# Summing 32,768 rows on one core: the first row joins a six-row load, narrower matmul pieces, the result stored in two parts from one partition

## The chip, the cores and the metric

The kernel runs on one core of one Trainium2 chip. The metric is the device time of an execution in microseconds; smaller is better. Medians are compared only with the kernel before on the same chip and in the same rounds. The profiled execution shows a span of its own, some 2 us shorter than the device time.

## The reference, cut to what matters

```python
def setup_inputs():
    batch, seq, dim = 32, 1024, 2048
    return {"grad_output": np.random.randn(batch, seq, dim).astype(np.float32)}

def reference(grad_output):
    return np.sum(grad_output, axis=(0, 1)).astype(np.float32)
```

32,768 rows of 2048 fp32 values are summed to one row. In the kernel a "row" is a block of 128 array rows, one on each partition (1 MB); there are 256 of them.

## The kernel before

The vector engine folds thirty 8-row tiles into a few rows in SBUF. The tensor engine adds up the partitions of what is left, with a column of ones as the stationary operand, into PSUM; it also takes the last rows straight from their loads: the vector engine is busy with the others without a pause from 567.16 to 618.00 us (trace). All loads are issued by one queue, in this order (a lane is the place of one row in the ring buffer):

```python
LEFT = ((0, 512, 0), (512, 512, 1), (1024, 512, 2))     # first column, columns, strip of the array
RIGHT = ((1536, 256, 2), (1792, 256, 3))
...
load(1, head[:], head_in)                               # one row first, for the vector engine
for k in range(TILES):                                  # 30 tiles of 8 rows, three buffers
    s = k % SLOTS
    load(TILE, rows(s * TILE, TILE), slot_in[s], (vec, k - 2) if k >= SLOTS else None)
load(1 + LANES, rows(0, 1 + LANES), rows_in, (vec, TILES - 2))   # five rows for the tensor engine
load(SMALL, rows(small_at, SMALL), small_in, (vec, TILES - 1))   # four rows for the vector engine
for j in range(LANES):
    load(1, rows(j, 1), row_in[j], (used, j + 1))       # one row each, once the lane is given back
...                                                     # then two rows, left columns before right
```

The tensor engine's program is 44 matmuls: one row, a loop body of four rows (run twice), the vector engine's sum, and the two last rows. A row is one matmul per piece; in the loop each row has a filler matmul besides, whose result is not used.

```python
matmuls(LANES * D, LEFT + RIGHT, wait=(rows_in, 16), start=True)
with nc.tensor.Fori(0, ROUNDS):
    for j, lane in enumerate(row_in):
        take(nc.tensor, lane)
        nc.tensor.matmul(psum[96:97, 1024:1024 + FILLER], ...)      # filler
        matmuls(j * D, LEFT + RIGHT).then_inc(used, 1)
matmuls(at * D, LEFT + RIGHT, wait=(step, n_step))
for x, lo, pieces, lane, stop in final:
    matmuls(x, pieces, lo, wait=(lane, 16), then=...)
```

Then the sums are copied out of PSUM and stored, left on partitions 0, 32 and 64, right on partition 96, by one DMA of four 2 KB pieces.

## Time and profile before

| | before |
|---|---|
| median of the first three runs | 629.28 us |
| span of the profiled run | 627.5 us |
| DMA engines taken | 99.1% |
| vector engine busy | 532.3 us |
| last load landed (trace) | 623.25 us |
| store started / landed (trace) | 624.46 / 626.22 us |

How to read it: the DMA engines are full from 2 us to 622 us, so the time is that of 268 MB plus a start of 2 us and an end of 4 to 5 us. "Landed" is the moment at which the sixteenth increment of a load's completion semaphore is recorded (each load gets sixteen; that each comes from another of the 16 DMA engines is assumed).

### The profile page before, as it was taken

How to read it: one execution, taken by the hardware profiler on the slowest of the kernel's cores; microseconds unless marked ns; L12 is line 12 of the kernel's file. 1: busy time of each engine (PE TensorE's matmuls, PEld its weight loads, DVE VectorE, ACT ScalarE, POOL GpSimd, SP SyncE). 2: the span in 40 equal slices, each digit the busy share in tenths (PEclk: the TensorE clock that was granted, in tenths of full speed). 3: DMA queues.
4: the chain of work that ended last, by engine and by line, in shares of the span. 5: the costliest groups of instructions: out<-in, count | busy, mean ns of one | idle time of the engine just before them, and what ended most of it. 6: DMA issues, size and time to landing. Idle time of an engine off the chain costs nothing. (4 is left out here: it accounts for less than half of the span.)

```text
span 627.5 us, 575 instructions
## 1 busy us (share of the span) xinstructions
PE 18.2 (3%) x136; PEld 4.9 (1%) x136; DVE 532.3 (85%) x68; ACT 2.4 (0%) x4; POOL 0.3 (0%) x5
## 2 busy tenths in 40 slices
PE   0000000000000000000000000000000000000055
PEld 0000000000000000000000000000000000000011
DVE  0349988889888898888988889988889888898994
ACT  0000000000000000000000000000000000000000
POOL 0000000000000000000000000000000000000000
PEclk9999999999999999999999999999999999999999
DMA  9999999999999999999999999999999999999996
GB/s 401 401 468 401 468 401 468 401 468 401 468 401 468 401 468 401 468 401 468 401 464 405 455 414 447 422 439 430 426 443 426 443 414 455 405 464 401 442 416 279
DMA packets 5912, 268.45 MB, mean 428 GB/s; under 512 B 660, under 2 KB 660, under 8 KB 1176
## 3 DMA queue, kind: packets, MB, share of 16 engines
q1 hardware_dynamic: 5912, 268.45, 99.1%
HBM read 268.44 MB, written 0.01 MB: 428 GB/s over the span
## 5 line engine op out<-in xcount | busy, mean ns | idle before, releaser
L118 DVE TENSOR_TENSOR ring<-ring 128x8192 f32<-128x8192 f32 (+2 forms) x65 | 528.6, 8134 | 84.9 <-DVEq L112 82.1
L183 PE MATMUL psum<-ring,ones 128*1 128x512 f32 (+1 forms) x120 | 18.2, 560 | 598.6 <-DMA ring<-in_grad_output_dram 598.5
L183 PEld LDWEIGHTS psum<-ring,ones 128*1 128x1 f32 x120 | 4.3, 86 | 608.4 <-DMA ring<-in_grad_output_dram 600.5
L200 PE MATMUL psum<-ring,ones 128*1 128x256 f32 x16 | 5.3, 412 | 7.0 <-PEq L112 7.0
L215 DVE COPY ring<-psum 1x256 f32<-1x256 f32 x1 | 0.4, 424 | 5.9 <-PE psum L183 5.9
L213 ACT COPY ring<-psum 96x512 f32<-96x512 f32 x1 | 0.6, 582 | 620.8 <-PE psum L183 620.8
L118 DVE TENSOR_TENSOR ring<-ring,head 128x2048 f32<-128x2048 f32 x1 | 2.3, 2292 | 0.1
L131 DVE MEMSET psum<- 128x1024 f32 x1 | 0.9, 912 | 1.2 <-SPq L121 1.2
L200 PEld LDWEIGHTS psum<-ring,ones 128*1 128x1 f32 x16 | 1.3, 92 | 10.0 <-issue 9.8
L211 ACT ACT_TABLE_LOAD x1 | 1.3, 1283 | 0.9 <-SPq L121 0.9
L216 ACT COPY ring<-psum 1x256 f32<-1x256 f32 x1 | 0.4, 365 | 0.3 <-PE psum L183 0.3
L211 ACT COPY warm<-ones 1x1 f32<-1x1 f32 x1 | 0.2, 190 | 0.0
L238 POOL MEMSET const-bfloat16-1.0<- 128x1 bf16 x1 | 0.1, 102 | 0.0
L238 POOL MEMSET const-uint8-127<- 128x1 uint8 x1 | 0.1, 102 | 0.0
L125 POOL MEMSET ones<- 128x1 f32 x1 | 0.1, 99 | 0.5 <-SPq L121 0.5
L238 POOL MEMSET const-float32-0.0<- 128x1 f32 x1 | 0.1, 99 | 0.2 <-issue 0.2
L238 POOL MEMSET const-float32-1.0<- 128x1 f32 x1 | 0.1, 99 | 0.0
## 6 DMA issues: line engine op xcount, KB each, us to landing
ring<-in_grad_output_dram SPq DMA_DIRECT2D x1, 5120.0 KB, 22.6
ring<-in_grad_output_dram SPq DMA_DIRECT2D x1, 4096.0 KB, 14.7
ring<-in_grad_output_dram SPq DMA_DIRECT2D x4, 1024.0 KB, 9.5
ring<-in_grad_output_dram SPq DMA_DIRECT2D x2, 768.0 KB, 13.5
head<-in_grad_output_dram SPq DMA_DIRECT2D x1, 1024.0 KB, 4.8
ring<-in_grad_output_dram SPq DMA_DIRECT2D x2, 256.0 KB, 14.5
ring<-in_grad_output_dram SPq DMA_DIRECT2D x30, 29.8
out_dram<-ring SPq DMA_DIRECT2D x1, 8.0 KB
```

Source lines behind the costliest of these rows:

```text
L118: return nc.vector.tensor_add(out=rows(at, n), in0=rows(at, n), in1=other)
L125: nc.gpsimd.memset(ones[:], 1.0).then_inc(one, 1)
L131: nc.vector.memset(psum[:, : 2 * 512], 0.0).then_inc(zero, 1)
L183: mat = nc.tensor.matmul(sums[lo], lhsT=ones[:], rhs=ring[:, x : x + n], start=start, stop=then is not None)
L200: nc.tensor.matmul(psum[96:97, 2 * 512 : 2 * 512 + FILLER], lhsT=ones[:], rhs=rows(j, 1)[:, :FILLER], start=True, stop=True)
L211: nc.scalar.copy(out=warm[:], in_=ones[0:1, :])._wait_ge(one, 1)
L213: nc.scalar.copy(out=res[:96, :], in_=psum[:96, :512])._wait_ge(mm_left, len(LEFT)).then_inc(left, 1)
L215: nc.vector.tensor_copy(out=half[:, 0, :], in_=sums[RIGHT[0][0]])._wait_ge(mm_right, 1).then_inc(right_0, 1)
L216: nc.scalar.copy(out=half[:, 1, :], in_=sums[RIGHT[1][0]])._wait_ge(mm_right, 2).then_inc(right_1, 1)
L238: nc = _bacc.Bacc("TRN2", target_bir_lowering=False, num_devices=1)
```

## The change

Its intent: a balanced last row (four left pieces of 416 and 352 columns in place of three of 512), the left three quarters stored while the right quarter is still being summed, and one small load and one vector add fewer at the start.

```diff
-LEFT = ((0, 512, 0), (512, 512, 1), (1024, 512, 2))
+LEFT = ((0, 416, 0), (416, 416, 1), (832, 352, 2), (1184, 352, 3))
...
-    load(1, head[:], head_in)
...
-    load(1 + LANES, rows(0, 1 + LANES), rows_in, (vec, TILES - 2))
+    load(MORE + LANES, rows(0, MORE + LANES), rows_in, (vec, TILES - 2))     # MORE = 2
...
-    matmuls(LANES * D, LEFT + RIGHT, wait=(rows_in, 16), start=True)
+    for i in range(MORE):
+        matmuls((LANES + i) * D, LEFT + RIGHT, wait=None if i else (rows_in, 16), start=i == 0)
...
-    res = ring[:, res_at : res_at + 512]
-    nc.scalar.copy(out=res[:96, :], in_=psum[:96, :512])._wait_ge(mm_left, len(LEFT)).then_inc(left, 1)
...
+    res = ring[0:1, res_at : res_at + D]
+    for copy, half in ((nc.scalar.copy, 0), (nc.vector.tensor_copy, 1)):
+        for i in range(2):
+            lo, n, _ = LEFT[2 * half + i]
+            result(copy, lo, n, (mm_left, len(LEFT)), left[half])
+        lo, n, _ = RIGHT[half]
+        result(copy, lo, n, (mm_right, half + 1), right[half])
+    nc.sync.wait_ge(left[0], 2)
+    nc.sync.dma_start(out=out[None, :cut], in_=res[:, :cut])._wait_ge(left[1], 2).then_inc(done, 16)
+    nc.sync.wait_ge(right[0], 1)
+    nc.sync.dma_start(out=out[None, cut:], in_=res[:, cut:])._wait_ge(right[1], 1).then_inc(done, 16)
```

More of the change, by code (lines that the diff above doesn't have):

```diff
@@ L19 @@
 LANES = 4
+MORE = 2
 SMALL = 4
@@ L44 @@
     R = flat.shape[0]
-    assert (1 + TILE * TILES + 1 + LANES * ROUNDS + SMALL + LAST) * P == R
+    assert (TILE * TILES + MORE + LANES * ROUNDS + SMALL + LAST) * P == R
     assert TILES == SLOTS * (LOOPS + 1)
@@ L51 @@
     ring = const_pool.tile([P, SLOTS * TILE * D], fp32)
-    head = const_pool.tile([P, D], fp32)
     ones = const_pool.tile([P, 1], fp32)
@@ L55 @@
     psum = psum_pool.tile([P, 3 * 512], fp32)
-    names = ("one", "zero", "vec", "step", "used", "mm_left", "mm_right", "left", "right_0", "right_1", "done")
-    one, zero, vec, step, used, mm_left, mm_right, left, right_0, right_1, done = (tc.alloc_semaphore(n) for n in names)
+    names = ("one", "zero", "vec", "step", "used", "mm_left", "mm_right", "done")
+    one, zero, vec, step, used, mm_left, mm_right, done = (tc.alloc_semaphore(n) for n in names)
     slot_in = [tc.alloc_semaphore(f"slot{s}") for s in range(SLOTS)]
@@ L65 @@
     last_in = [tc.alloc_semaphore(f"last{i}") for i in range(2 * LAST)]
-    head_in = tc.alloc_semaphore("head")
+    left = [tc.alloc_semaphore(f"left{i}") for i in range(2)]
+    right = [tc.alloc_semaphore(f"right{i}") for i in range(2)]
     def rows(at, m):
@@ L133 @@
     vadd(0, rows(WIDE, WIDE), WIDE)
-    nc.vector.wait_ge(head_in, 16)
-    settle()
-    vadd(0, head[:], 1)
     with nc.vector.Fori(0, LOOPS):
@@ L211, with result @@
     nc.scalar.copy(out=warm[:], in_=ones[0:1, :])._wait_ge(one, 1)
-    res = ring[:, res_at : res_at + 512]
-    nc.scalar.copy(out=res[:96, :], in_=psum[:96, :512])._wait_ge(mm_left, len(LEFT)).then_inc(left, 1)
-    half = res[96:97, :].rearrange("p (h n) -> p h n", h=2)
-    nc.vector.tensor_copy(out=half[:, 0, :], in_=sums[RIGHT[0][0]])._wait_ge(mm_right, 1).then_inc(right_0, 1)
-    nc.scalar.copy(out=half[:, 1, :], in_=sums[RIGHT[1][0]])._wait_ge(mm_right, 2).then_inc(right_1, 1)
-    nc.sync.wait_ge(left, 1)
-    nc.sync.wait_ge(right_0, 1)
-    nc.sync.dma_start(out=out.rearrange("(g n) -> g n", g=4), in_=res[0:128:32, :])._wait_ge(right_1, 1).then_inc(done, 16)
+    res = ring[0:1, res_at : res_at + D]
+    def result(copy, lo, n, wait, then):
+        copy(out=res[:, lo : lo + n], in_=sums[lo])._wait_ge(*wait).then_inc(then, 1)
+    for copy, half in ((nc.scalar.copy, 0), (nc.vector.tensor_copy, 1)):
[8 more added lines that the diff above has]
+    nc.sync.dma_start(out=out[None, cut:], in_=res[:, cut:])._wait_ge(right[1], 1).then_inc(done, 16)
     section.__exit__(None, None, None)
     with tc.tile_critical(no_gpsimd_drain=True):
-        nc.sync.wait_ge(done, 16)
+        nc.sync.wait_ge(done, 32)
 _INS = ['grad_output']
```

## The prediction

> **What bounds the kernel now.** I read the page's busy rows and queue row first, then the chain that ended last, then the timeline of the last 30 us, the queue's own waits, and the stretch table of the last microseconds.
>
> The page says that memory is the bound:
>
> ```profile
> DMA  9999999999999999999999999999999999999996
> ...
> q1 hardware_dynamic: 5912, 268.45, 99.1%
> ...
> HBM read 268.44 MB, written 0.01 MB: 428 GB/s over the span
> ```
>
> The row of tenths is full until the last slice, and the 16 DMA engines are taken 99.1% of the span. One 8-row tile is 8.389 MB. The vector engine starts an add on a fresh tile at 25.27 us and, 28 tiles later, at 567.16 us (timeline), so a tile takes (567.16 - 25.27) / 28 = 19.353 us, which is 433 GB/s. The vector engine is busy 532 us of 627 and waits 82.1 us for tiles. It is second. So whatever leaves the number of bytes as it is can act only before the stream starts (about 1.5 us), in a hole in the stream, or after its end. The end is the second half of this chain:
>
> ```profile
> 606.89 0.33 SPq L106
> ...
> 607.74 14.21 DMA ring<-in_grad_output_dram
> 621.95 0.04 issue
> 622.00 1.95 PE psum L183 x13
> 623.95 0.40 DVE ring L215
> ```
>
> Up to 621.95 the chain is a load in a full queue. Then come 1.95 us of matmuls, a copy out of PSUM, and what follows in the timeline:
>
> ```profile
> 622.00 0.10 PEld L183 LDWEIGHTS psum<-ring,ones 128*1 128x1 f32 x6 [1.01 <-DMA ring<-in_grad_output_dram]
> 622.66 0.29 PEld L183 LDWEIGHTS psum<-ring,ones 128*1 128x1 f32 x4 [0.56 <-DMA ring<-in_grad_output_dram]
> 623.14 0.58 ACT L213 COPY ring<-psum 96x512 f32<-96x512 f32 x1 [620.75 <-PE psum L183]
> ...
> 623.93 0.42 DVE L215 COPY ring<-psum 1x256 f32<-1x256 f32 x1 [5.93 <-PE psum L183]
> 623.97 0.36 ACT L216 COPY ring<-psum 1x256 f32<-1x256 f32 x1 [0.25 <-PE psum L183]
> 624.46 0.65 SPq L219 DMA_DIRECT2D out_dram<-ring  x1
> ```
>
> The reader is to see that the six weight loads at 622.00 belong to the left part of the last row (three pieces, two instructions each), that the left copy at 623.14 is hidden behind the matmuls of the right part, and that the single store starts 0.11 us after the later of the two right copies (623.93 + 0.42 = 624.35). The store's instruction takes 0.65 us. Its packets show between 625.5 and 626.0 in the stretch table, and the queue then waits 0.2 us for it among the closing barriers; 627.5 is the end. From the store's start to the end of the span is 3.0 us.
>
> [...]rows of matmuls follow each other at 603.67 minus 602.38 = 1.29 us when data is there; a row puts 512, 512, 768 and 512 columns (the last with the filler) on the four strips, and 768 columns in 1.29 us is 1.68 ns a column, while all 2304 one after another would need 3.9 us. [...]
>
> **The change part by part.**
>
> *The single first row goes; the tensor engine's first load takes six rows.* Bytes stay. A row loaded alone is paced at (618.30 - 610.82) / 3 = 2.49 us (the tensor engine's waits for the four late rows), against 19.353 / 8 = 2.42 us inside a tile, so one separate load costs about 0.07 us of stream. Merging it saves about 0.05 us. The vector engine loses one add of 2.29 us and gets every tile 2.4 us earlier. It runs without a pause from 567.16 to 618.0, and its sum is not read before row four's matmuls end at 619.6, so this is only slack: worth 0.
>
> *One more row of matmuls before the four lanes are given back.* With the new cuts the strips hold 416, 416, 352 + 256 = 608, and 608 columns, the last 864 with the filler. So a row with filler costs 864 x 1.67 = 1.44 us (was 1.28) and one without 1.01 us. Before, the first lane was given back at 603.02, when 2 rows of 768 were done: 4.48 us after 598.54, of which 1536 x 1.67 = 2.56 us is at full pace and 1.92 us is start-up. After, strip four has 3 x 608 + 256 = 2080 columns: 3.47 + 1.92 = 5.39 us, so 603.9; the others follow at 605.4, 606.8 and 608.3 (was 606.89). The queue is fed until the four-row load lands, at 593.52 + 14.7 = 608.2 us, so the first row load comes 4.3 us early and the fourth, whose turn is near 615.6, comes 7 us early. No hole: worth 0.
>
> *The end.* The left part of the last row lands near 621.95 as before. Its matmuls took 512 x 1.67 = 0.85 us plus 0.29 us to the copy's start. Now they take 416 x 1.67 = 0.69, so the left copies start at 622.98 instead of 623.14. The right part ended by strip three: (512 + 256 + 256) x 1.67 = 1.71 us; now (352 + 256 + 256) x 1.67 = 1.44 us, 0.27 us sooner, 623.66 instead of 623.93. The last data is in at 622.8, in time:
>
> ```profile
> 622.60:622.70 0.10, 0.10 (x5) 0.04 (x3) 0.00 (x0) 0.00 (x0) 0.00 (x0) 1.00 0.17 62
> 622.70:622.80 0.10, 0.10 (x4) 0.05 (x3) 0.00 (x0) 0.00 (x0) 0.00 (x0) 1.00 0.06 21
> 622.80:623.00 0.20, 0.20 (x6) 0.08 (x1) 0.00 (x0) 0.00 (x0) 0.00 (x0) 1.00 0.00 0
> ```
>
> (Columns: stretch, length, busy time and count of PE, weight loads, DVE, ACT, POOL, then clock, DMA share, GB/s.) But the copies now bind, not the matmuls. Each engine has three in a row. The scalar engine's cost is 582 ns for 512 columns and 365 ns for 256, so 0.85 ns a column, 501 ns for 416. The vector engine's is 424 ns for 256, and at 1.04 ns a column 524 ns for 352. With 0.05 us between two copies (my choice; no row shows two of them back to back): scalar 622.98, 623.53, 624.08 to 624.45; vector 622.98, 623.55, 624.13 to 624.55. So the PE's 0.27 us is lost and the right half is ready at 624.55, 0.20 us later than before. The left half is ready at 624.08, and its store starts 0.11 us later, at 624.19. If it takes 0.65 us like the old one, the queue is free at 624.84 and the right store starts at 624.88, 0.42 us later than the old store. If a store over 16 engines takes 0.33 us, as the loads do (0.33 at 606.89), the right store starts at 624.66, 0.20 us later, but its own instruction is 0.32 us shorter, so it ends 0.12 us earlier than the old one. I give the first 60%, the second 40%: 0.6 x 0.42 - 0.4 x 0.12 = +0.20 us.
>
> Sum: -0.05 + 0 + 0 + 0.20 = +0.15 us; 629.28 + 0.15 = 629.43, say 629.4.
>
> **The rivals.** First, *the early store pays*: what is stored last is 2 KB instead of 8, its instruction is short, the copies overlap at their ends, and the tail shrinks by 0.3 to 0.5 us: 628.9. For it: the tensor engine does end earlier, and the load instructions are half as long as the store. Against it: three copies a side in place of one or two, and a second issue on one queue. Second, *the stores become the bound*: the left store holds the queue for 0.65 us and the right store's small pieces on 16 engines land later than four pieces of 2 KB: +0.6 us, 629.9. For it: 0.65 us is the only duration of a store that this trace has. Third, *the stream gets a hole*, because the row loads wait for one more row of matmuls[...]: each microsecond past the 4.3 us of slack would be paid in full, 630 or more. Against it: the slack is three times the delay. Fourth, *the vector engine was the bound* and freeing it gains up to 2.3 us: 627. Against it: 82.1 us of waits for tiles, and a DMA row with no slice under nine before the last.
>
> **Range and chances.** The first two rivals give 628.9 and 629.9; the runs of before spread over 0.4 us. A range of 628.8 to 630.0 holds these. The third and fourth together get some 5%. Two per cent is 12.6 us, thirty times any term here: 1% faster, 98% within, 1% slower.
>
> **What would show each step.** Right if the queue is still near 99% busy at 433 GB/s; if the last LDWEIGHTS group waits for a load near 622; if the row loads issue near 603.9 and 608.3; if the first copy starts near 623.0, the last ends near 624.5, and the right store starts after 624.6. The early store's step is wrong if the right store starts before 624.5. A last load landing a microsecond later would mean a hole; one landing earlier would mean that the start, which I took as equal, counts for more. A vector engine that ends after 619.7 would show the fourth rival.

The 1.67 ns a column of the matmuls is close to the 1.68 of the trace (1.29 us a row over the fullest strip's 768 columns). That the fullest strip sets a row's time, and not its 2304 columns, the changed kernel's trace shows as well: the same 2304 columns, with 864 on the fullest strip, follow each other at 1.46 us (604.84 to 606.30), again some 1.68 ns. The 1.04 ns a column of the vector engine's copies was measured on no copy before; its adds in the same trace give it ((8692 - 4424) ns over 8192 - 4096 columns). And a store split over 16 engines, in the 40% case and in the second rival, was an assumption that no trace showed.

## The result, and the profile after

| | before | changed |
|---|---|---|
| median of six runs | 629.31 us (629.18 to 629.69) | 630.27 us (630.13 to 630.71) |
| ratio | | 1.0015, 95% interval 1.0002 to 1.0028 |

A ratio is the mean time of one kernel's fast runs over that of the other's of the same rounds, so it is not quite the ratio of the medians. By the 2% measure this is "the same"; by microseconds it is 0.96 us slower, where 0.15 had been predicted, and outside the range.

The queue part of the page of the changed kernel has two lines more than before; the one for queue 8 matters here:

```profile
q1 hardware_dynamic: 5764, 268.45, 98.9%
q8 instruction: 1, 0.02, 0.0%
...
HBM read 268.44 MB, written 0.01 MB: 427 GB/s over the span
```

The columns are packets, MB and share. One packet of 16 KB went over a queue of kind "instruction" within the span. Its share rounds to nothing.

The end of the changed kernel's timeline (start, length, engine, line, instruction, and in brackets the idle time before it and what ended it; PE is the tensor engine, PEld its weight loads, ACT the scalar and DVE the vector engine, SPq the issuing of a DMA):

```profile
622.68 0.10 PEld L179 LDWEIGHTS psum<-ring,ones 128*1 128x1 f32 x8 [1.12 <-DMA ring<-in_grad_output_dram]
623.36 0.09 PEld L179 LDWEIGHTS psum<-ring,ones 128*1 128x1 f32 x4 [0.57 <-DMA ring<-in_grad_output_dram]
623.71 1.02 ACT L211 COPY ring<-psum 1x416 f32<-1x416 f32 x2 [621.33 <-PE psum L179]
623.71 1.08 DVE L211 COPY ring<-psum 1x352 f32<-1x352 f32 x2 [5.68 <-PE psum L179]
624.82 0.32 SPq L221 DMA_DIRECT2D out_dram<-ring  x1
625.34 0.09 PEld L179 LDWEIGHTS psum<-ring,ones 128*1 128x1 f32 x4 [1.89 <-DMA ring<-in_grad_output_dram]
625.97 0.36 ACT L211 COPY ring<-psum 1x256 f32<-1x256 f32 x1 [1.25 <-PE psum L179]
626.01 0.43 DVE L211 COPY ring<-psum 1x256 f32<-1x256 f32 x1 [1.23 <-PE psum L179]
626.47 0.25 SPq L223 DMA_DIRECT2D out_dram<-ring  x1
```

Two things are to be seen. The left part of the last row arrives at 622.68 where it was 622.00 before: the stream is 0.7 us late. And the tensor engine waits 1.89 us for the very last load, which let it start at 625.34; before, the same group followed at 623.29. The two right copies stand idle behind it, although the left copies had been done at 624.79. The chain of waits says the same: its last load now ends at 625.30.

```profile
610.60 14.70 DMA ring<-in_grad_output_dram
625.30 0.04 issue
625.34 0.65 PE psum L179 x4
625.99 0.02 issue
626.01 0.43 DVE ring L211
```

The sixteen increments of that last load, from the trace: fifteen are there between 623.55 and 623.94, the sixteenth at 625.30. The packet records of those microseconds show what lies between (start in us, length, queue, bytes):

```
623.098    11 ns   q1       4     semaphore of an earlier load
623.113  1101 ns   q8   16384     instruction
624.200    24 ns   q1       4     the last load's sixteenth semaphore
```

The records name the queue but not the engine, so that these three went over one engine is inferred from their times: the semaphore packet starts only as the 16 KB end, it takes 24 ns where others take 9 to 14, and only one increment is late. Nor does the packet's own delay make up the whole: from its start to its increment it takes 1.10 us, where the last packet before it (623.471) and the fifteenth increment are 0.47 us apart. So some 0.6 of the 1.36 us lie between packet and increment, and no record shows why.

The accounts of the two profiled runs, from the trace:

| | before | changed | difference |
|---|---|---|---|
| left part of the last row in, PE starts | 622.00 | 622.68 | +0.68 |
| last load landed | 623.25 | 625.30 | +2.05 |
| last store started | 624.46 | 626.47 | +2.01 |
| last store landed | 626.22 | 627.61 | +1.39 |
| span | 627.54 | 628.93 | +1.39 |

So 0.7 us are lost in the stream, another 1.36 us by one late semaphore, and 0.62 us are won in the store: its start-to-landing time is 1.14 us where the old one's was 1.76. This profiled run is the slowest of the changed kernel's six; the others have spans of 628.4 to 628.7. In it, tiles 1 to 4 come 19.37 to 19.77 us apart (by their sixteenth increments) in place of 19.35, and from tile 5 on the pace is that of before. How much of the 0.7 us other runs lose can't be read from their times alone.

### The profile page after: what moved, and what is told of

Read it like the earlier page. It is cut to its first block, busy times and chain, and to the rows that moved or that the text cites. A ratio compares the mean times of both kernels' runs of the same rounds, so it can differ in the third digit from the quotient of the medians.

```text
span 628.9 us, 649 instructions
## 1 busy us (share of the span) xinstructions
PE 20.8 (3%) x172; PEld 7.5 (1%) x172; DVE 531.1 (84%) x69; ACT 2.8 (0%) x5; POOL 0.3 (0%) x5
## 5 line engine op out<-in xcount | busy, mean ns | idle before, releaser
L179 PE MATMUL psum<-ring,ones 128*1 128x352 f32 (+2 forms) x156 | 20.8, 514 | 601.1 <-DMA ring<-in_grad_output_dram 601.1
L179 PEld LDWEIGHTS psum<-ring,ones 128*1 128x1 f32 x156 | 7.0, 88 | 611.0 <-DMA ring<-in_grad_output_dram 602.8
L211 DVE COPY ring<-psum 1x352 f32<-1x352 f32 (+1 forms) x3 | 1.5, 490 | 6.9 <-PE psum L179 6.9
L211 ACT COPY ring<-psum 1x416 f32<-1x416 f32 (+1 forms) x3 | 1.4, 452 | 622.6 <-PE psum L179 622.6
L197 PEld LDWEIGHTS psum<-ring,ones 128*1 128x1 f32 x16 | 1.1, 82 | 7.0 <-issue 6.3
```

The costliest lines, as they stand in the source:

```text
L179: mat = nc.tensor.matmul(sums[lo], lhsT=ones[:], rhs=ring[:, x : x + n], start=start, stop=then is not None)
L197: nc.tensor.matmul(psum[96:97, 2 * 512 : 2 * 512 + FILLER], lhsT=ones[:], rhs=rows(j, 1)[:, :FILLER], start=True, stop=True)
L211: copy(out=res[:, lo : lo + n], in_=sums[lo])._wait_ge(*wait).then_inc(then, 1)
```

## The experiments

Two theories were set against each other. **Fetch**: the sixteenth semaphore is late because 16 KB of the tensor engine's program are fetched by the same DMA engine just before it, and the fetch is there because the program got longer. **Store**: the new end itself (narrow pieces, two stores) delays the last load's semaphore. Apart from that, the 0.7 us in the stream wanted a cause. In every comparison the median of the kernel before is that of the same batch. The 95% intervals of the ratios include 1 in experiments 1 to 3, 7 to 12, 14 and 15 (for example 0.9973 to 1.0006 in experiment 1). In experiments 1, 8, 10 and 12 all runs are nevertheless faster than all runs of before; in 2, 3, 14 and 15 the runs overlap with those of before, so that the few tenths of these four are differences of medians and no more.

### 1. The first row restored (undo_first)

```diff
-MORE = 2
+MORE = 1
+    load(1, head[:], head_in)
+    vadd(0, head[:], 1)          # after a wait on head_in, as before
```

> The changed kernel with the single first row restored (one row of matmuls fewer, five rows in the first load); narrower pieces and the two stores kept. Theory (fetch): the late last landing of the changed kernel (625.30 where its 15 neighbours are in by 623.94) comes from the 16 KB instruction fetch at 623.11, which is there because the tensor engine's program grew from 44 to 58 matmuls; with 52 it should come after the last load, so the last landing is level and the right store starts about 1.1 us after the left one's copies, some 0.4 us earlier than before: 628.8 to 629.0 if the 0.7 us lost in the first tiles goes with the single row as well. Rival (store): the new end itself makes the last landing late: 630.0 or more, with a late last landing again.

Measured: 628.78 us against 629.46, 0.68 us faster than before, four runs from 628.65 to 628.78. With 52 matmuls the last load is level: all sixteen increments come between 622.70 and 623.10. The end of its timeline:

```profile
622.86 1.41 ACT L217 COPY ring<-psum 1x416 f32<-1x416 f32 x3 [620.48 <-PE psum L185]
622.86 1.42 DVE L217 COPY ring<-psum 1x352 f32<-1x352 f32 x3 [5.00 <-PE psum L185]
623.14 0.09 PEld L185 LDWEIGHTS psum<-ring,ones 128*1 128x1 f32 x4 [0.55 <-DMA ring<-in_grad_output_dram]
623.97 0.32 SPq L227 DMA_DIRECT2D out_dram<-ring  x1
624.40 0.25 SPq L229 DMA_DIRECT2D out_dram<-ring  x1
```

The three copies of each engine run back to back, and the second store starts at 624.40. The narrow pieces and the two stores are all there, so the store theory falls. But the fetch theory's expectation was not met to the letter either: the fetch is still within the span, at 622.461, and does no harm. It begins 6 ns after the start of a semaphore packet. Four 2 KB pieces (the last at 622.527) and eight semaphore packets (the last at 622.607) begin after it; all take their usual 84 and 9 ns, and none waited for it.

### 2. The six-row load alone (only_first)

```diff
-    load(1, head[:], head_in)
-    load(1 + LANES, rows(0, 1 + LANES), rows_in, (vec, TILES - 2))
+    load(MORE + LANES, rows(0, MORE + LANES), rows_in, (vec, TILES - 2))
+    # and MORE = 2 rows of matmuls ahead of the loop; pieces and store as before
```

> The kernel before with the first row's load removed and six rows in the first load of the tensor engine; old pieces, old store. If the 0.7 us lost between 42 and 101 us belongs to the stream that begins with an 8-row tile: 630.0, with tiles 1 to 4 spaced over 19.4 us. If that loss was chance: 629.3, tiles all spaced 19.35 us. Fetch theory: 49 matmuls, so no fetch before the end.

Measured: 629.79 against 629.46, but four runs from 629.55 to 630.77, far more spread than before's 0.4 us. The profiled run lost about 0.15 us in tiles 3 to 5. The fetch is there with 49 matmuls, against the expectation, at 622.749, 6 ns after the start of a semaphore packet, and all of the last load is in by 623.47. That the run at 630.77 was one in which it came sooner would fit, but only the profiled run has a trace.

### 3. Six-row load and two stores, old pieces (first_store)

```diff
+    copies: ACT 512, 512 and 256 columns, DVE 512 and 256, all to partition 0
+    dma_start(out[None, :cut], res[:, :cut]);  dma_start(out[None, cut:], res[:, cut:])
```

> As the run with six rows alone, plus the result on one partition and two stores, but the old three left pieces of 512 (49 matmuls). Fetch theory: no fetch in the end; the store on one engine lands 1.1 to 1.3 us after its start where the old one took 1.76, the right copies end near 0.3 us later than before: 0.2 to 0.4 us faster than the run with six rows alone. Rival (store): a late last landing and 630 or more.

Measured: 629.59 (629.07 to 629.84) against 629.46, 0.20 us under the run with six rows alone. The fetch is within the span again (622.937), and again none of the last load waits for it. The store lands 1.15 us after its start. (That the new store is one engine's and the old one four engines' is inferred, as the records name no engine: in the changed kernel's trace each store is one packet, in before's it is four that overlap in time, from 625.70 to 625.89.) One engine is 0.5 us behind the others from the first one-row load on; section "why" comes back to that.

### 4. The kernel before with a longer program (before_pad14)

```diff
     nc.tensor.wait_ge(zero, 1)
+    for _ in range(14):
+        nc.tensor.matmul(psum[96:97, 1024:1025], lhsT=ones[:], rhs=ones[:], start=True, stop=True)
```

> The kernel before with 14 matmuls of one column at its start, where the tensor engine has nothing to do for 590 us: 58 matmuls in the program, as in the changed kernel, and nothing else. Fetch theory: the 16 KB fetch moves from after the end into the last loads, and the last landing of one engine comes 1 to 1.4 us late: 630.2 to 630.7. Rival (store, or chance): no change, 629.3.

Measured: 630.60 against 629.46, runs from 630.53 to 630.92. Nothing but 14 matmuls (56 instructions) was added, done by 3.2 us, and the kernel is 1.14 us slower. Its page and its timeline have what the changed kernel's have:

```profile
q8 instruction: 1, 0.02, 0.0%
```

```profile
624.52 0.09 PEld L183 LDWEIGHTS psum<-ring,ones 128*1 128x1 f32 x4 [1.53 <-DMA ring<-in_grad_output_dram]
...
625.68 0.64 SPq L221 DMA_DIRECT2D out_dram<-ring  x1
```

Fifteen increments of the last load come by 623.30, the sixteenth at 624.48. The fetch goes from 622.298 to 623.397. After its start come two pieces of the last load of 231 and 227 ns (at 623.383 and 623.600), where such 2 KB pieces otherwise take 84 to 96 ns, and then the late semaphore packet at 623.813. So it is not always the semaphore alone that is late; here an engine's last pieces are, too. The edit touches the tensor engine's program alone, and the fetch comes with it: this run settles the fetch theory for the late landing.

### 5 and 6. The changed kernel with a still longer program (after_pad28, after_pad54)

```diff
+    for _ in range(28):          # 54 in the second
+        nc.tensor.matmul(psum[96:97, 1024:1025], lhsT=ones[:], rhs=ones[:], start=True, stop=True)
```

> The changed kernel with 28 matmuls of one column ahead of its first wait, so that the program's length at any later point is 112 instructions more. Fetch theory: the 16 KB fetch [...]moves to the first pass of the row loop, near 603 to 608 us, and the last landing is level again; what the fetch takes from one engine there (up to 1.1 us) can either come out at the end or be caught up: 628.7 to 629.9, below the changed kernel's 630.3. Rival (store or narrow pieces make the last landing late): 630.3 with the same late landing.

> As the run with 28, but 54: [...] Fetch theory: the fetch shows in the first microseconds, the end has none: 628.7 to 629.9. [...]

Measured: 630.44 and 630.90 against 629.33. The fetch moved as expected, to 605.475 and to 10.288 us. The lost time did not go. From the fetch on, one increment of every load is about 1.2 us late (with 54 until the hole named below). With 54, tile 0 has fifteen increments between 22.27 and 23.09 and the sixteenth at 24.25, and tile 29, 560 us later, fifteen by 584.24 and the sixteenth at 585.41. With 28, the last load has fifteen by 623.72 and one at 624.88, and the left part of the last row fifteen by 622.44 and one at 623.63, which the tensor engine waits for:

```profile
623.68 0.10 PEld L179 LDWEIGHTS psum<-ring,ones 128*1 128x1 f32 x8 [1.11 <-DMA ring<-in_grad_output_dram]
```

So both expectations missed, in one point: what the fetch takes from an engine is never caught up in these traces, whose DMA engines are taken 99.0%. The fetch costs about 1.2 us here at 10, at 605 and at 623 us alike. The run with 54 has a second fetch after the last load, and a hole in its row loads besides (below). Its runs go from 630.18 to 631.71; the slowest has the same span as the profiled run (628.7 us, at 630.47), so that what sets it apart lies outside the span and isn't explained.

### 7. The first tile in two parts (after_split)

```diff
-    load(TILE, rows(0, TILE), slot_in[0])          # k = 0
+    first row of the tile (1 MB), semaphore first_in;  the other seven (7 MB), slot_in[0]
```

> The changed kernel with its first tile loaded in two parts, one row (1 MB) first and seven rows (7 MB) after it, on two semaphores; all else as changed, the fetch included. Theory: a stream that begins with 64 KB pieces loses 0.15 to 0.7 us in the first five tiles, one that begins with a 1 MB load of 8 KB pieces doesn't: all tiles spaced 19.35 us, and 0.2 to 0.7 us less than the changed kernel: 629.6 to 630.0. Rival (what counts is the address of the tiles, 1 MB further on before, or chance): a loss in the first tiles again, 630.3.

Measured: 630.22 against 629.33. The early tiles of the profiled run lose again, 0.8 us in all, with the tiles up to 19.81 us apart. A small first load is no cure. The profiled run is the slowest of four (629.80 to 630.90), and whether the two at 629.8 lost there isn't known.

### 8. Two stores alone (only_store)

```diff
     pieces, first row and loads as before
+    copies and the two stores as in experiment 3
```

> The kernel before with the result on one partition and two stores alone: first row, three left pieces of 512 and 44 matmuls as before. The right store should start 0.3 to 0.4 us later than the old store's 624.46 (the scalar engine has copies of 512, 512 and 256 columns) and land 1.14 us after its start in place of 1.76: 0.2 to 0.3 us faster than before, with the fetch after the end: 629.1. Rival (the one-engine store is slower than four engines): 629.8.

Measured: 629.00 against 629.33, 0.33 us faster, runs within 0.14 us. No fetch in the span. In its timeline the longest copies end at 624.65, later than before's 624.35, yet the kernel is faster:

```profile
624.35 0.32 SPq L222 DMA_DIRECT2D out_dram<-ring  x1
624.78 0.25 SPq L224 DMA_DIRECT2D out_dram<-ring  x1
```

### 9 and 10. Where the tiles lie (after_shift, head_unshift)

```diff
 after_shift: the changed kernel
-    at_row = 0
+    at_row = P                     # the last row is taken from the array's first 1 MB
 head_unshift: experiment 1
-    load(1, head[:], head_in)
+    load(1, head[:], head_in, first=R - P)
```

> The changed kernel with every load moved by 128 rows (1 MB) in the array, as the loads stood before, and the very last row taken from the array's first 1 MB; no single first row. Theory (address): the 0.15 to 0.9 us that the streams without a first row lost in their early tiles comes from where the tiles lie; then all tiles are 19.35 us apart here and the time is 0.2 to 0.7 us under the changed kernel's 630.3: 629.6 to 630.0, the late last landing still there. Rival (order): a stream that begins with a tile loses the same again wherever it lies: 630.2, early tiles of 19.4 to 19.8 us.

> The changed kernel with a single first row restored, but that row is the array's last, so the tiles begin at the array's start, as in the changed kernel. Theory (address): early tiles of 19.4 to 19.8 us, 629.0 to 629.4. Rival (order): all tiles 19.35 us apart, 628.8, as the run with the first row restored at its own place.

Measured: 629.98 and 628.85, against 629.30 (a median of seven; one of these took 632.90, at a granted clock of 0.98 where the others had 0.993 to 0.997). The shifted kernel's profiled run has no loss in the early tiles and the late landing (fifteen by 623.37, one at 624.70). The other has none of both. Taken alone, the first seems to favour the address and the second the order. With the later traces neither holds: see below.

### 11 and 12. Versions that beat both kernels (undo_first_nofill, undo_first_again)

```diff
 undo_first_nofill: experiment 1
-FILLER = 256
+FILLER = 0
 undo_first_again: experiment 1, unchanged, on another chip
```

> The version with the first row restored and, besides, no filler matmuls in the row loop: 48 matmuls. Fetch theory: with 44 to 48 the fetch comes after the last loads or not before the end at all, well clear of the last semaphore, where with 52 it came 6 ns after it. [...]628.8 if the clock holds, 629.6 to 630.2 if it falls.

> The version with the first row restored, once more on this chip: 628.6 to 628.9 if its gain of 0.7 us over before is not that chip's. If the fetch's place against the last semaphore is a matter of chance, some runs near 630.

Measured: 628.91 and 628.85, against 629.30. The repeat had runs from 628.64 to 629.08. Both have medians under the kernel before, by 0.4 to 0.45 us here and 0.68 in experiment 1, some 0.1%. Without the filler the slowest run (629.18) reaches into the runs of before (from 629.15); in experiments 1 and 12 none does. The fetch came at 623.300 without the filler, after all semaphore packets of the last load, and at 622.844 with it. Both profiled runs lost a little in the early tiles (0.3 and 0.1 us), with the single first row in place. That the clock would fall without the filler was the assumption, and no fall shows: the runs of experiment 11 had granted clocks of 0.991 to 0.995 (0.997 to 1.0 with the filler, experiment 12), and the left copies start 1.02 us after the tensor engine took up the left part, against 1.03 us with it (the changed kernel).

### 13 to 15. The six-row load at a shorter program

```diff
-FILLER = 256
+FILLER = 0        # in the changed kernel, in experiment 2 and in experiment 3
```

> The changed kernel without its filler matmuls, 54 in the program in place of 58. Fetch theory: at 49 and 52 the fetch began after the last semaphore of its engine and did no harm, at 58 before the last pieces; with 54 it can fall either way. If it falls after: 628.8 plus what the six-row load itself costs (0 to 0.6). If before: 630.2 with one late last landing.

> The kernel before with the six-row load alone and no filler: 45 matmuls, so no fetch near the end. If the six-row load costs nothing of its own: 629.3, as before. If it costs by losses in the early tiles: 629.5 to 630.0, with tiles over 19.4 us apart in the trace.

> The six-row load and the two stores with the old three left pieces and no filler: 45 matmuls. If the six-row load costs nothing of its own: 629.0, as the two stores alone. If it costs: 629.2 to 629.7.

Measured: 630.34, 630.03 and 629.53, against 629.28. With 54 matmuls the fetch is again before the last pieces (622.667; fifteen increments by 623.71, one at 625.00). With 45 there is none, and still the six-row load costs: 0.75 us alone, and 0.25 us with the two stores, which without it gain 0.33. Runs spread over 0.7 and 0.9 us. The two profiled ones lost nothing in the early tiles.

Taken together, the tensor engine's program and the fetch:

| matmuls in the program | kernels | fetch in the profiled run | harm |
|---|---|---|---|
| 44 | before, only_store | none in the span (before: one at 629.35, after it) | none |
| 45 | only_first_nofill, first_store_nofill | none | none |
| 48, 49 | undo_first_nofill, only_first, first_store | 622.7 to 623.3 | none |
| 52 | undo_first (twice), head_unshift | 622.4 to 622.8 | none |
| 54 | after_nofill | 622.667 | 1.3 us |
| 58 | changed, after_shift, after_split, before_pad14 | 622.3 to 623.3 | 1.2 to 1.4 us |
| 86 | after_pad28 | 605.475 | 1.2 us |
| 112 | after_pad54 | 10.288 | 1.2 us |

What decides between harm and none at 48 to 58 seems to be a few tenths of a microsecond: whether the fetch begins before or after the last load's pieces on its engine. As the engine isn't recorded, this is an inference. Counted back from the last load's fifteenth increment, the fetch begins 0.30 to 0.86 us before it in the six traces without harm and 0.83 to 1.05 us in the five with harm; and in five of the six without harm it begins 6 ns after the start of a semaphore packet, in none of the others. With 86 and 112 matmuls it comes far earlier; from 48 to 58 its times overlap.

## Why the prediction was right or wrong

**The bound and the mechanism of the end were right.** Queue near 99%, 19.35 us a tile, vector engine second and no cause of anything. Where the trace has a number for a step, it is close: copies of 416 and 352 columns took 496 and 522 ns (501 and 524 predicted), with 0.03 us between them (0.05); the left copies started 1.03 us after the tensor engine took up the left part (0.98 predicted); the first row load was issued at 604.44 (603.9) and the fourth at 608.81 (608.3).

**The step that failed is "The last data is in at 622.8, in time".** It was read off the profile of before and carried over. In the changed kernel the last load landed at 625.30, and the right half waited for it. The last 2 KB piece of the changed kernel is in by 623.48, but the kernel waits for sixteen increments, and the sixteenth came 1.36 us after the fifteenth (625.30; the tensor engine went on at 625.34). No term of the sum stood for the length of the program, although the change adds 14 matmuls to it in plain sight. The prediction said that "A last load landing a microsecond later would mean a hole"; it landed later without one. Experiment 4 shows the missing term alone, +1.14 us on the kernel before.

**"Sum: -0.05 + 0 + 0 + 0.20" began with a gain that wasn't there.** Merging the single row was to save 0.05 us. At program lengths where no profiled run shows harm from the fetch, the six-row load cost, by medians, 0.33 us (experiment 2), 0.75 (13 to 15, alone), and with the two stores 0.46 and 0.58 (0.13 + 0.33 and 0.25 + 0.33 us, across two batches). The traces show two places where it went, in some runs and not in others:

- *Early tiles.* Taking the middle one of the sixteen increments, tile 29 less tile 0 less 29 times 19.353 us, over 0.1 us were lost in 5 of 10 traces without a single first row (0.15 to 0.78 us) and in 2 of 7 with one (0.11 and 0.29). Order, address and the size of the first piece were each tried, and each had a counterexample. The cause of this loss stays open.
- *A hole at the first one-row load.* This was the third rival, and the prediction took 4.3 us of slack for safe. The slack (issue of the first row load to the earliest landing of the load before it) was 4.65 us before and 4.05 in the changed kernel, where the trace shows no hole. In experiments 3 and 14 it was 2.84 and 2.63, and some engines had 2.7 to 3.1 us between two landings where 2.48 is the pace; in experiment 6 it was 1.51, with a mean of 3.0. With a slack of 2.61 experiment 2 had none, and none of the others, from 3.06 up, had one. So the direction of the third rival was right and shows at the edges; it is not what made the changed kernel slow.

**The store was mis-sized, in the other direction.** The prediction gave 60% to stores of 0.65 us and wrote that this was "the only duration of a store that this trace has". They took 0.32 and 0.25 us. From its start the last one landed in 1.13 to 1.15 us in all 13 traces of kernels with two stores, against 1.75 to 1.77 in the four with the old one. In place of "0.6 x 0.42 - 0.4 x 0.12 = +0.20 us", the end gave back 0.4 to 0.7 us (experiments 1, 11 and 12), 0.33 of it by the stores alone (experiment 8). The first rival, the early store that pays, was thus right about the end, and its gain was hidden under the fetch. And the split over 16 engines, to which the prediction gave 40%, did not happen: each store is one packet, of 6144 and of 2048 bytes.

**So the sum in terms of what the runs show.** The end: -0.4 to -0.7 us. The fetch: +1.2 to +1.4. The six-row load in the stream: 0 to +0.8 by the run. Together +0.5 to +1.8, measured +0.96.

## What to carry to other kernels

When a change adds instructions to an engine's program, look in the trace for a packet on a queue of kind "instruction" (16 KB here), and for where in time it falls: on this kernel, whose DMA engines are taken 99%, 14 matmuls more brought one into the last load and cost 1.14 us (experiment 4), and it was free only where, as far as the traces tell, it came after its DMA engine's last piece. When the last wait of a kernel is for a load, look at all sixteen increments of its semaphore and at the queues of kind "instruction", not only at when the bytes came; and when two parts of a change act on the same end, run each alone, because here a gain of half a microsecond was hidden under a loss of more than one.
